# A transposed copy of the lower 16x16 inverse, made once on ScalarE, in the 32x32 inverses of a gated DeltaNet mixer

## The chip, the cores and the metric

The kernel runs on one core of a Trainium2 chip. The metric is the device time of one execution in microseconds (us). The core has five engines, each with its own queue, worked off strictly in order: PE (TensorE, the matmuls), DVE (VectorE), ACT (ScalarE), POOL (GpSimd) and SP, which here only issues DMAs. An instruction whose inputs are not there yet holds up everything behind it on its engine.

## The reference

One encoder layer for two sequences, of 2048 and 512 tokens. The input projection is cut into four mixers (spatial gating, gated DeltaNet, attention, pooling), each is gated, and an output projection follows. The change sits in the DeltaNet mixer. For every chunk of 64 tokens, head and direction, that mixer needs the inverse of a unit lower triangular matrix:

```python
lower = jnp.where(strict, jnp.einsum("bnhid,bnhjd->bnhij", k_beta, k) * decay, 0.0)
t_mat = lax.linalg.triangular_solve(lower + eye, jnp.broadcast_to(eye, lower.shape),
                                    left_side=True, lower=True, unit_diagonal=True)
u = t_mat @ v_beta
w = t_mat @ (k_beta * jnp.exp(g)[..., None])
...
def step(state, xs):
    w_c, u_c, q_c, k_c, a_c, gl_c = xs
    v_new = u_c - w_c @ state
    out = q_c @ state + a_c @ v_new
    state = state * jnp.exp(gl_c)[..., None, None] + jnp.einsum("bhcd,bhce->bhde", k_c, v_new)
    return state, out
```

## The kernel before

The 2560 tokens are worked in five blocks of 512, each of four tiles of 128. `phase1` projects and convolves. Then three things share the engines: the DeltaNet (`deltanet`), the rest of the projections (`phase2`, two passes, matmuls named `accq`, `accz` and `accu`), and, once the pools of the DeltaNet's front are free, attention with the output projection (`phase3`). The program is written unit by unit, and a scheduler with a timeline of its own then sets one order for each engine, by priorities (the DeltaNet's is high) and by when it thinks things are ready. So a change in one place can move rows far behind it, on every engine.

The DeltaNet of a block runs like this, with a tile of 128x128 couplings for each head and direction:

- `pre` (lines 1070 to 1133), once per tile: PE makes the decay exponents `gp` (L1095, L1099) and the key products `kk` (L1110), ACT takes the exponential into `dt` (L1102), DVE makes the couplings `nl` (L1114) and the scaled `dt` (L1116). The 32x32 diagonal blocks go out to DRAM as `dg`. POOL finishes the part `at` (L1131).
- `lanes` (lines 1135 to 1165), once per block: the 128 diagonal blocks of 32x32 are loaded back so that each partition holds one of them, flattened to 1024 values, in the tile `lnl` (`nf`, seen as `nl[p, a, b]`). The inverse grows in the tile `lx` (`xf`, seen as `xt`), which POOL first sets to the identity (L1146, L1147). All products are the helper `dot`: one DVE multiplication into `ltmp` (L1153) and one DVE reduction along the last axis (L1154). First the two 16x16 inverses on the diagonal grow in 15 steps. Then the block `z` that couples them is made: 4 dots that multiply rows of couplings (from `lnl`) with rows of the upper inverse, and 4 dots that multiply the result with the lower inverse, both operands from `lx`. These last four have 1024, 768, 512 and 256 products. A DMA writes the result to DRAM as `xl` (L1165).
- `levels` (from line 1168), twice per block: loads `xl` (L1179), turns it (L1183, L1191), and merges 32x32 blocks to 64 and 128 with small matmuls.
- `step` (in `recurrence`): the state recurrence. Forward and backward direction are two independent chains per sequence. On DVE a step shows as L1289 to L1291, L1296, L1302, L1307, L1314 and L1284.

The upper right quarter of `nl`, `nl[:, 0:16, 16:32]`, is loaded with the rest but no dot reads it: couplings there are zeros.

Two norms feed the same queues: `norm_sums` (L613, L616), whose reciprocal root is POOL's (`rsqrt_pool`, L66 to L71, split at L92), and `norm_turn` (L626).

Of the kernel before, what the change touches and what calls it, by code (L numbers as in the profile page):

```python
# [10 lines left out]
AF = mybir.ActivationFunctionType  # L11
# [33 lines left out]
class Trunk:  # L45
# [1022 lines left out]
    def front(self, dp, dq):  # L1068

        nc = self.nc  # L1070
        V, A, G, PE = nc.vector, nc.scalar, nc.gpsimd, nc.tensor
# [63 lines left out]
        def lanes(tds):  # L1135
            L = len(tds) * 16
            b = tds[0][0] // 4
            done.append(b)
            nf = dp.tile([128, 1056], F32, tag="lnl", name="lnl", bufs=1)
            xf = dp.tile([128, 1056], F32, tag="lx", name="lx", bufs=1)  # L1140
            sq = lambda t: t[:, 0:1024].rearrange("p (a b) -> p a b", b=32)
            halves = lambda t: t.rearrange("p (h x) -> p h x", x=528)[:, :, 0:512].rearrange(
                "p h (a b) -> p h a b", b=32)[:, :, :, 0:16]
            nl, xt, nh, xh = sq(nf), sq(xf), halves(nf), halves(xf)
            nc.sync.dma_start(nf[:, 0:1024], self.DG[b])
            G.memset(xf, 0.0)  # L1146
            G.memset(xf[:, 0:1024:33], 1.0)  # L1147

            def dot(out, x, y, shape):
                tmp = dp.tile([128, 1024], F32, tag="ltmp", name="ltmp", bufs=1)  # L1150
                n = shape[1] * shape[2] * shape[3]
                t = tmp[:, 0:n].rearrange("p (a b c) -> p a b c", a=shape[1], b=shape[2])
                V.tensor_tensor(t, x.to_broadcast(shape), y.to_broadcast(shape), op=ALU.mult)  # L1153
                V.tensor_reduce(out, t, axis=AX.X, op=ALU.add)  # L1154


            for i in range(1, 16):
                dot(xh[:, :, 0:i, i], xh[:, :, 0:i, 0:i], nh[:, :, i:i + 1, 0:i], [128, 2, i, i])
            z = xt[:, 0:16, 16:32]
            for k in range(0, 16, 4):  # L1160
                dot(z[:, k:k + 4, :], nl[:, 16:32, k:16].unsqueeze(1), xt[:, k:k + 4, k:16].unsqueeze(2), [128, 4, 16, 16 - k])
            for k in range(12, -4, -4):
                w = xt[:, 16:20 + k, 16 + k:20 + k].rearrange("p b a -> p a b")
                dot(z[:, :, k:k + 4], w.unsqueeze(1), z[:, :, 0:k + 4].unsqueeze(2), [128, 16, 4, k + 4])
            nc.sync.dma_start(self.XL[b], xf[:, 0:1024])  # L1165

        def levels(t):
# [70 lines left out]
            for d, Pr, Sr in ends:  # L1238
# [5 lines left out]
                for j in range(2):  # L1244
                    nc.sync.dma_start(self.TT[t + j][d], t16[:, :, j * 4:j * 4 + 4].rearrange("p i u f -> p i (u f)"))

        return pre, lanes, levels


# [236 lines left out]
```

## Time and profile before

| | us |
|---|---|
| three timed runs | 1581.16, 1572.33, 1577.47 (median 1577.47) |
| the profiled execution, its own time | 1574.01 |
| its span, first to last instruction | 1572.2 |
| 0 to 340: `phase1` | PE 317.20 busy of 340 |
| 340 to 840: the five `lanes`, with `phase2` beside them | PE 427.10, DVE 405.70 busy of 500 |
| 840 to 1093: end of the recurrence, begin of attention | PE 227.36, DVE 210.82 busy of 253 |
| 1093 to 1500: attention and output projection | PE 386.56, DVE 311.21 busy of 407 |

How to read it: a busy time close to a stretch's length says that the engine sets the pace there, or that it is nearly full. Where no engine is full, the pace is set by waits of one queue for another; such a row shows its idle time and what ended it in brackets, `[2.36 <-DVE dt L1116]`.

### The profile page before, as it was taken

The numbers are of one execution on the slowest core, as the hardware profiler recorded it, in microseconds if no ns is written. First come the engines' busy times: TensorE is split into PE (matmuls) and PEld (weight loads), VectorE is DVE, ScalarE is ACT, GpSimd is POOL, SyncE is SP. The second block draws the span as 40 slices with busy tenths as digits, with TensorE's granted clock in tenths as the row PEclk, the third lists the DMA queues.
The fourth block names the chain that finished last, engine by engine and source line by source line (L and its number), as shares of the span: only waits on it lengthen the run. The fifth ranks groups of instructions, "written<-read, shape, count | busy, mean of one in ns | idle before, by whom it ended". The sixth has DMA issues, their size and how long they took to land. (4 is left out here: it accounts for less than half of the span.)

```text
span 1572.2 us, 34743 instructions
## 1 busy us (share of the span) xinstructions
PE 1425.8 (91%) x13420; PEld 783.5 (50%) x13420; DVE 1173.3 (75%) x2265; ACT 797.0 (51%) x1655; POOL 546.7 (35%) x646
## 2 busy tenths in 40 slices
PE   6999999988989887987889879998799999999898
PEld 3456555543444443544445435555355555555443
DVE  6338579967969887996957769998877887877611
ACT  5244444545454844554546215565567675576400
POOL 3220220044748643455453435555121221121100
PEclk9999999998899989989999999999799999999999
DMA  9845643556566877657689885644411501414332
GB/s 254 283 168 168 190 151 114 150 194 193 160 186 201 258 234 218 199 171 215 186 259 311 278 255 177 202 139 148 161 48 39 173 34 65 160 33 135 114 128 107
DMA packets 250830, 269.65 MB, mean 172 GB/s; under 512 B 95784, under 2 KB 176680, under 8 KB 250024
## 3 DMA queue, kind: packets, MB, share of 16 engines
q1 hardware_dynamic: 250264, 267.36, 54.1%
q8 instruction: 105, 1.72, 0.4%
q14 instruction: 61, 0.50, 0.1%
q0 software_dynamic: 400, 0.07, 0.1%
HBM read 175.66 MB, written 91.77 MB: 170 GB/s over the span
## 5 line engine op out<-in xcount | busy, mean ns | idle before, releaser
L127 PEld LDWEIGHTS <-w 128*128 128x128 f16 x2280 | 223.5, 101 | 307.5 <-issue 81.8
L127 PE MATMUL accz<-xs,w 128*128 128x512 f16 x960 | 243.7, 402 | 16.8 <-DMA xs<-xs 6.7
L958 PE MATMUL op<-wo,mx 128*128 128x512 f16 x960 | 225.3, 379 | 1.0 <-DVE y L962 1.0
L886 DVE TENSOR_REDUCE mm<-mp 128x1 f32<-128x512 f32 x272 | 179.5, 683 | 52.4 <-PE mp L884 52.1
L916 POOL TENSOR_TENSOR p<-e,p 128x512 f16<-128x512 f32 x68 | 86.7, 1274 | 318.6 <-ACT p L915 283.7
L912 ACT ACTIVATE e<-sp 128x512 f32<-128x512 f32 x272 | 153.4, 596 | 79.3 <-PE sp L910 72.9
L916 DVE TENSOR_TENSOR p<-e,p 128x512 f16<-128x512 f32 x204 | 165.8, 828 | 19.3 <-ACT p L915 19.1
L127 PE MATMUL acc<-xs,w 128*128 128x512 f16 x720 | 162.8, 383 | 3.8 <-POOL xs L291 1.5
L915 ACT ACTIVATE p<-e 128x512 f16<-128x512 f32 x272 | 161.2, 632 | 3.4 <-PE O L921 2.0
L921 PEld LDWEIGHTS <-p 128*128 128x128 f16 x3264 | 128.1, 97 | 55.8 <-DVE p L916 11.2
L921 PE MATMUL O<-vt,p 128*128 128x65 f16 (+1 forms) x3264 | 142.6, 193 | 7.5 <-DVE p L916 5.3
L958 PEld LDWEIGHTS <-mx 128*128 128x128 f16 x960 | 91.3, 98 | 104.4 <-issue 1.8
L884 PE MATMUL mp<-ka,qa 128*128 128x512 f16 x272 | 98.7, 395 | 17.3 <-DVE mm L886 10.6
L909 PE MATMUL sp<-qa,ka 128*128 128x512 f16 x272 | 103.9, 384 | 2.6 <-ACT e L912 1.2
L306 DVE SCALAR_TENSOR_TENSOR cv<-raw,convw,cv 128x512 f32<-128x512 f32 x120 | 88.0, 754 | 21.2 <-POOL raw L382 20.6
L910 PE MATMUL sp<-qb,kb 65*128 65x512 f16 x272 | 100.5, 387 | 1.2 <-ACT qb L894 1.0
L127 PE MATMUL accq<-xs,w 128*128 128x512 f16 x360 | 89.5, 391 | 9.9 <-DMA xs<-xs 7.0
L400 PE MATMUL acct<-wtm,xs 128*128 128x400 f16 x480 | 83.8, 332 | 1.9 <-ACT ba L408 0.9
L1268 POOL TENSOR_TENSOR kd<-kv,kds 128x512 f16<-128x512 f32 x40 | 46.9, 1179 | 108.0 <-PE up L1305 56.0
L291 POOL TENSOR_TENSOR xs<-xt,xs 128x512 f16<-128x512 f32 x36 | 49.1, 1386 | 73.5 <-ACT xs L288 73.2
L962 DVE SCALAR_TENSOR_TENSOR y<-op,xr 128x512 f32<-128x512 f32 x40 | 27.5, 687 | 59.2 <-PE op L958 59.1
L127 PE MATMUL accu<-xs,w 128*128 128x512 f16 x240 | 60.9, 403 | 7.2 <-DVE s L616 7.0
(316 smaller groups left out, 2506.8 us busy)
## 6 DMA issues: line engine op xcount, KB each, us to landing
xs<-xs SPq DMA_DIRECT2D x120, 256.0 KB
kx<-kx SPq DMA_DIRECT2D x80, 256.0 KB
at<-at SPq DMA_DIRECT2D x80, 256.0 KB
tt<-tt SPq DMA_DIRECT2D x80, 256.0 KB
xt<-in_xT SPq DMA_DIRECT2D x40, 256.0 KB
xs<-xs SPq DMA_DIRECT2D x5, 2048.0 KB
kv<-kv SPq DMA_DIRECT2D x40, 256.0 KB
mix<-mixs SPq DMA_DIRECT2D x40, 256.0 KB
```

Source lines behind the costliest of these rows:

```text
L127: mm = self.nc.tensor.matmul(ps, w[:, a, k, :], xk, start=k + i == 0, stop=k == 7 and i == 2)
L306: V.scalar_tensor_tensor(cv, raw[:, ct, i:i + 512], self.convw[:, ct, i:i + 1], cv, op0=ALU.mult, op1=ALU.add)
L400: PE.matmul(acc[:, 0:400], xs[:, a, k, tt * 128:(tt + 1) * 128], w[:, c, k, :], start=n == 0, stop=n == 23)
L884: PE.matmul(mp, qa[:, qt * 128:qt * 128 + 128], KA[h // 2][:, sc * 512:sc * 512 + 512], start=True, stop=True)
L886: V.tensor_reduce(mm[:, qt, sc:sc + 1], mp, axis=AX.X, op=ALU.max)
L909: PE.matmul(sp, KA[kv][:, c], qa, start=True, stop=False)
L910: PE.matmul(sp, KB[kv][:, c], qb, start=False, stop=True)
L912: A.activation(e, sp, AF.Exp)
L915: A.activation(p[:, 0], e, AF.Copy)
L916: (G if st % E8 == 1 else V).tensor_tensor(p[:, 1], e, p[:, 0], op=ALU.subtract)
L921: mm = PE.matmul(O[:, qt, 0:z - a], p[:, w, q], v[:, a:z], start=st == 0 and qt == 0 and i == 0, stop=st == nst - 1 and i == 2, skip_group ...
L958: PE.matmul(op, mix[k][:, a, tt * 128:tt * 128 + 128], wo[k][:, c, n * 512:n * 512 + 512], start=i + j == 0, stop=i == 7 and j == 2)
```

## The change

After the four dots that make the first half of `z`, one ACT instruction copies the lower 16x16 inverse, transposed, into the unused quarter of `nl`. The four dots behind it then read the copy `w2` along its rows instead of reading `xt` down its columns. It happens once per block, five times in all.

```diff
             for k in range(0, 16, 4):
                 dot(z[:, k:k + 4, :], nl[:, 16:32, k:16].unsqueeze(1), xt[:, k:k + 4, k:16].unsqueeze(2), [128, 4, 16, 16 - k])
+
+            w2 = nl[:, 0:16, 16:32]
+            A.activation(w2, xt[:, 16:32, 16:32].rearrange("p b a -> p a b"), AF.Copy)
             for k in range(12, -4, -4):
-                w = xt[:, 16:20 + k, 16 + k:20 + k].rearrange("p b a -> p a b")
+                w = w2[:, k:k + 4, 0:4 + k]
                 dot(z[:, :, k:k + 4], w.unsqueeze(1), z[:, :, 0:k + 4].unsqueeze(2), [128, 16, 4, k + 4])
             nc.sync.dma_start(self.XL[b], xf[:, 0:1024])
```

Behind the new lines the line numbers of the changed kernel are higher by three (L1102 stays, L1186 becomes L1189).

ACT in the first of the five blocks, before. The rows belong to `pre` of the following block, and `zz` is a gate of `phase2`:

```order
L1130 ACTIVATE at_4906<-dt 128x512
L606 ACTIVATE zz<-accz 128x512
L1102 ACTIVATE dt<-gp,lcj 128x128 x8
L1130 ACTIVATE at_4962<-dt 128x512
L1126 ACTIVATE dg<-nl 32x128 x4
```

The same place after:

```order
L1130 ACTIVATE at_4907<-dt 128x512
L606 ACTIVATE zz<-accz 128x512
L1102 ACTIVATE dt<-gp,lcj 128x128 x8
L1164 ACTIVATE lnl<-lx 128x16x16
L1130 ACTIVATE at_4963<-dt 128x512
L1126 ACTIVATE dg<-nl 32x128 x4
```

The copy stands between the exponentials and a row that waits for DVE; nothing else moved. In the first three blocks DVE's rows keep their places too; only the names of what four rows read change.

From the fourth block on, rows move on all engines. DVE at the beginning of the fifth `lanes` (rows of `lx` and `ltmp`), with the norms and rotations of `phase2` and steps of the recurrence beside it, before:

```order
L1302 TENSOR_TENSOR v_7486<-up,v_7486 128x256
L1153 TENSOR_TENSOR ltmp<-lx,lnl 128x2
L1154 TENSOR_REDUCE lx<-ltmp 128x2
L616 TENSOR_SCALAR s<-ssp 128x16
L697 TENSOR_TENSOR rt<-q,cs 128x512
L1153 TENSOR_TENSOR ltmp<-lx,lnl 128x8
L66 TENSOR_SCALAR r<-s 128x16
L1307 SCALAR_TENSOR_TENSOR S<-up,S 128x256
L699 TENSOR_TENSOR q<-q,cs 128x512
L700 TENSOR_TENSOR q<-q,rt 128x512
L1154 TENSOR_REDUCE lx<-ltmp 128x2x2
```

and after:

```order
L1153 TENSOR_TENSOR ltmp<-lx,lnl 128x2
L1154 TENSOR_REDUCE lx<-ltmp 128x2
L1305 TENSOR_TENSOR v_7489<-up,v_7489 128x256
L1153 TENSOR_TENSOR ltmp<-lx,lnl 128x8
L1154 TENSOR_REDUCE lx<-ltmp 128x2x2
L1153 TENSOR_TENSOR ltmp<-lx,lnl 128x18
L1154 TENSOR_REDUCE lx<-ltmp 128x2x3
L1153 TENSOR_TENSOR ltmp<-lx,lnl 128x32
L1154 TENSOR_REDUCE lx<-ltmp 128x2x4
L1186 STREAM_TRANSPOSE tnd<-d_8203 128x256
```

The dots of the fifth block have moved ahead of the norm's `s` and the rotations.

DVE some hundred rows later, behind the last `lanes`, with the recurrence's two directions side by side (`S`, `o`, `s` of each), gates (`gz`) and the weights of the output projection (`wo`), before:

```order
L1302 TENSOR_TENSOR v_8560<-up,v_8560 128x256
L1307 SCALAR_TENSOR_TENSOR S<-up,S 128x256 x2
L607 SCALAR_TENSOR_TENSOR gz<-gz,accz 128x512 x2
L1314 SCALAR_TENSOR_TENSOR o<-up,o 128x256
L860 SCALAR_TENSOR_TENSOR wo_12964<-wst,wo_12964 128x1024
L768 SCALAR_TENSOR_TENSOR gz<-ld,psc,gz 128x512
L1314 SCALAR_TENSOR_TENSOR o<-up,o 128x256
```

and after:

```order
L1305 TENSOR_TENSOR v_8564<-up,v_8564 128x256
L860 SCALAR_TENSOR_TENSOR wo_12969<-wst,wo_12969 128x1024
L860 SCALAR_TENSOR_TENSOR wo_12974<-wst,wo_12974 128x1024
L607 SCALAR_TENSOR_TENSOR gz<-gz,accz 128x512
L1310 SCALAR_TENSOR_TENSOR S<-up,S 128x256
L1292 TENSOR_TENSOR o<-up,neg_275 128x256
L1293 TENSOR_TENSOR kv_8610<-o,kv_8610 128x256
L768 SCALAR_TENSOR_TENSOR gz<-ld,psc,gz 128x512
L1294 TENSOR_TENSOR o<-up,eg_273 128x256
```

Before, the two directions update `S` in one go and both gates stand behind them; after, the directions alternate, and a gate stands ahead of the update. On PE the last matmul of the recurrence stands 469 rows earlier than before (row 13568 instead of 14037), with 602 instead of 768 of the attention's `O` matmuls ahead of it, while the first attention matmul stands 294 rows later (row 9902 instead of 9608).

## Prediction

> **What bounds the kernel now.** I read the page's busy times first, then the table by stretches, cut at the five `lanes` (first dot to the write of `xl`), then what PE waits for inside them.
>
> ```profile
> PE 1425.8 (91%) x13420; PEld 783.5 (50%) x13420; DVE 1173.3 (75%) x2265; ACT 797.0 (51%) x1655; POOL 546.7 (35%) x646
> ```
>
> Over the whole span PE is the fullest engine, so a shorter DVE instruction can bring something only where PE waits, directly or through others, for DVE. The stretches (length, then busy time of PE, its weight loads, DVE, ACT, POOL, then granted clock and DMA):
>
> ```profile
> 378.00:431.00 53.00, 47.82 (x242) 22.63 (x241) 50.13 (x98) 27.20 (x70) 32.77 (x44) 0.93 0.49 147
> 452.00:514.00 62.00, 52.37 (x621) 27.84 (x622) 59.73 (x106) 34.15 (x79) 44.81 (x57) 0.92 0.51 162
> 555.00:621.00 66.00, 52.16 (x478) 27.52 (x477) 59.39 (x117) 32.27 (x79) 30.12 (x37) 0.91 0.68 214
> 628.00:699.00 71.00, 64.06 (x839) 36.95 (x838) 66.02 (x140) 38.42 (x93) 35.31 (x55) 0.90 0.57 171
> 734.00:788.00 54.00, 47.02 (x571) 25.97 (x571) 52.26 (x93) 23.60 (x44) 26.51 (x37) 0.94 0.54 164
> 340.00:840.00 500.00, 427.10 (x4545) 226.51 (x4545) 405.70 (x799) 274.20 (x643) 264.69 (x373) 0.91 0.68 208
> 840.00:1093.00 253.00, 227.36 (x2828) 132.88 (x2827) 210.82 (x367) 123.65 (x246) 129.67 (x130) 0.97 0.67 214
> 1093.00:1500.00 407.00, 386.56 (x3957) 217.22 (x3956) 311.21 (x557) 247.07 (x462) 79.70 (x61) 0.97 0.29 97
> ```
>
> In the five `lanes` together DVE is busy 50.13 + 59.73 + 59.39 + 66.02 + 52.26 = 287.5 of 306 us, 94%; PE only 263.4, 86%. There DVE sets the pace. In 340 to 840 as a whole it is busy 81% and PE 85%: between the `lanes` other waits decide. From 1093 on PE is at 95% and takes over: what PE gains before that, it keeps to the end.
>
> That PE waits for DVE there is seen in its own rows; each of these stands behind one or more of the dots that the change shortens:
>
> ```profile
> 426.98 0.38 PE L1095 MATMUL gp<-negf,id 128*128 128x512 f16 x1 [2.36 <-DVE dt L1116]
> 512.85 0.39 PE L1095 MATMUL gp<-negf,id 128*128 128x512 f16 x1 [1.52 <-DVE dt L1116]
> 617.15 0.38 PE L1095 MATMUL gp<-negf,id 128*128 128x512 f16 x1 [0.91 <-DVE dt L1116]
> 692.85 0.39 PE L626 MATMUL turned<-id,r 128*12 128x128 f16 x4 [2.42 <-POOL r L92]
> 784.31 1.89 PE L127 MATMUL accu<-xs,w 128*128 128x512 f16 x8 [1.98 <-DVE s L616]
> ```
>
> **The dots.** The change keeps the number of DVE instructions and of products. What changes is how the last four multiplications of a block read one operand: now down a column, 32 numbers (128 bytes) apart, later along a row. The trace has both kinds in the same sizes, 20 of each: the first four dots of `z` read a row of `lnl` against a row of `lx`, with inner lengths of 16, 12, 8 and 4, as the last four will after the change. First the column readers (`lx` alone), then the row readers (`lnl,lx`):
>
> ```profile
> L1153 DVE TENSOR_TENSOR ltmp<-lx 128x1024 f32<-128x1024 f32 (+3 forms) x20 | 29.9, 1496 | 0.2
> L1153 DVE TENSOR_TENSOR ltmp<-lnl,lx 128x1024 f32<-128x1024 f32 (+3 forms) x20 | 19.0, 949 | 0.2
> 498.11 1.95 DVE L1153 TENSOR_TENSOR ltmp<-lx 128x1024 f32<-128x1024 f32 x1
> 612.51 1.46 DVE L1153 TENSOR_TENSOR ltmp<-lx 128x768 f32<-128x768 f32 x1
> 617.01 1.03 DVE L1153 TENSOR_TENSOR ltmp<-lx 128x512 f32<-128x512 f32 x1
> 697.37 0.59 DVE L1153 TENSOR_TENSOR ltmp<-lx 128x256 f32<-128x256 f32 x1
> 585.19 1.23 DVE L1153 TENSOR_TENSOR ltmp<-lnl,lx 128x1024 f32<-128x1024 f32 x1
> 588.76 0.95 DVE L1153 TENSOR_TENSOR ltmp<-lnl,lx 128x768 f32<-128x768 f32 x1
> 403.39 0.68 DVE L1153 TENSOR_TENSOR ltmp<-lnl,lx 128x512 f32<-128x512 f32 x1
> 601.23 0.41 DVE L1153 TENSOR_TENSOR ltmp<-lnl,lx 128x256 f32<-128x256 f32 x1
> ```
>
> By the two groups the saving is 29.9 - 19.0 = 10.9 us. But some of these rows were held up, and a held-up row need not get shorter:
>
> ```profile
> 423.43 1.25 POOL L644 TENSOR_TENSOR sh<-sg 64x512 f32<-64x512 f32 x1 [2.08 <-ACT dg L1126]
> 423.71 1.36 DVE L1153 TENSOR_TENSOR ltmp<-lx 128x256 f32<-128x256 f32 x1
> ```
>
> The dot of 256 products took 1.36 us here instead of 0.59, and about one microsecond of it lies under a POOL row. So the floor comes from the undisturbed rows: (1.95 - 1.23) + (1.46 - 0.95) + (1.03 - 0.68) + (0.59 - 0.41) = 1.76 us a block, 8.8 us in five. DVE saves 8.8 to 10.9 us; I take 9, near the floor. The Trainium skill, page "SBUF — State Buffer", section "Who interferes with whom", says that a DVE instruction with two SBUF inputs and a GpSimd instruction that reads SBUF exclude each other until the first is done. By that rule the hold-ups stay and the saving is the floor; by a rule of plain slowing it would be the 10.9. The two rows just shown agree with the first.
>
> **The copy.** ACT gets five instructions more, 128x256 in fp32, reading 128 bytes apart. No such row exists. The nearest is one of the same 256 elements along rows, 0.41 us; below that I see no reason, and if a column costs ACT what it costs DVE for the dot of 256 (0.59 to 0.41), it is 0.6 us. I take 0.5, together 2.5 us, all of it on an engine that is half idle. What counts is whether the dots wait for it. The copy can start when the last of the 15 steps has been reduced, and the first column reader comes later:
>
> ```profile
> L1195 ACT ACTIVATE tn<-d 32x256 f32<-32x256 f32 x20 | 8.2, 412 | 1.7 <-DMA d<-xl 1.4
> 396.33 0.62 DVE L1154 TENSOR_REDUCE lx<-ltmp 128x30 f32<-128x450 f32 x1
> 408.75 2.19 DVE L1153 TENSOR_TENSOR ltmp<-lx 128x1024 f32<-128x1024 f32 x1
> 405.15 0.63 ACT L1130 ACTIVATE at<-dt 128x512 f16<-128x512 f32 x1 [9.69 <-DVE dt L1116]
> 669.21 1.06 ACT L1242 ACTIVATE tt<-tt 128x1024 f16<-128x1024 f32 x1 [1.48 <-DMA tt<-tt]
> ```
>
> In the first block 408.75 - 396.95 = 11.8 us lie between, and ACT's order puts the copy into the 9.69 us that it idles ahead of `at`. The wait that the change adds is over long before DVE comes to it, and behind the copy on ACT stands a row that waits for DVE anyway: cost nothing. In the fourth block ACT has no such hole: behind the copy stand `z` of `levels` and eight exponentials, and the delay of 0.4 to 0.6 us ends at the idle 1.48 us before 669.21. Five times without any cover the copy would cost its 2.5 us and no more. I take 0.
>
> `lnl` is now needed until the last dot, not only until the fourth of `z`, and the next block's load may not overwrite it earlier. The tightest case is the fourth block's load:
>
> ```profile
> 618.80 1.32 DVE L1153 TENSOR_TENSOR ltmp<-lx 128x256 f32<-128x256 f32 x1
> 623.44 0.38 SPq L1145 DMA_DIRECT2D lnl<-dg  x1
> ```
>
> The last reader ends at 620.12, the load goes out 3.3 us later: cost nothing.
>
> **How much of 9 us reaches PE.** Per block I take the smaller of PE's idle time in the rows above and of what the dots ahead of it save: 1.76 (of 2.36); 1.52 (three dots ahead, 1.58); 0.91; 0.72 (only the first dot is ahead of the norm whose root POOL makes); 1.58 (of 1.98). Sum 6.5 us. Behind some of these waits another one is nearly as late, since POOL and ACT rows end there too; I take 5. It can't fall below 0 by itself, and 10.9 is the ceiling.
>
> **The order.** The rows for the third `lanes` and before are the old ones, so those terms are clean. From the fourth on the scheduler has placed rows anew: the recurrence finishes earlier on PE, attention begins later there, and on DVE the two directions no longer go in pairs. From 1093 on the rows are nearly the old ones, PE's total work is the same, so only idle time can change. Between 840 and 1093 that is 253 - 227.36 = 25.6 us, and between 340 and 840 it is 72.9 us. I take 0 for the move, with bounds from the rivals below.
>
> Sum: 1574.0 (the profiled execution's own time, 1572.2 span and 1.8 around it) - 5 = 1569.0. The median of the runs shown is 3.5 us higher than this execution; for a median I forecast 1569.0 + 3.5, rounded **1572**. About 0.5%, 7.9 us, is what a measurement of this kernel can tell from no change, and 5 us is less than that.
>
> **Rivals.** *Everything passes and the new order helps.* For it: DVE is 94% busy in the `lanes`, so all 9 to 10.9 us could shorten them, and the earlier dots release `xl`, `levels` and the steps too. And the old order has a knot that the new one unties:
>
> ```profile
> 820.46 0.84 DVE L1307 SCALAR_TENSOR_TENSOR S<-up,S 128x256 f32<-128x256 f32 x2 [2.70 <-PE up L1305]
> 826.36 1.28 DVE L607 SCALAR_TENSOR_TENSOR gz<-gz,accz 128x512 f32<-128x512 f32 x2 [5.05 <-ACT gz L606]
> 827.10 5.78 PE L127 MATMUL accz<-xs,w 128*128 128x512 f16 x19 [3.76 <-DVE gz L607]
> 849.82 0.75 DVE L1307 SCALAR_TENSOR_TENSOR S<-up,S 128x256 f32<-128x256 f32 x2
> ```
>
> There DVE waits 2.70 us for both directions' matmuls, then 5.05 for a gate, and PE loses 3.76. Against it: DVE's gaps between the `lanes` (94.3 - 18.5 = 76 us in 340 to 840) are other waits, which can take up a gain. With all 10.9 and up to 8 from untied knots: 1577.5 - 9 to 1577.5 - 19, so 1558 to 1568.
>
> *The new order costs more than the dots save.* Mechanism: recurrence steps stand closer on PE, while the chain of one step (matmuls, DVE, ACT, matmuls, DVE) needs its time. Above, two updates lie 29.4 us apart (820.46 to 849.82). The new order takes 166 of the attention's `O` matmuls, 42 projection and 25 score matmuls from ahead of the recurrence's last one. Their price by the page:
>
> ```profile
> L921 PE MATMUL O<-vt,p 128*128 128x65 f16 (+1 forms) x3264 | 142.6, 193 | 7.5 <-DVE p L916 5.3
> L127 PE MATMUL accz<-xs,w 128*128 128x512 f16 x960 | 243.7, 402 | 16.8 <-DMA xs<-xs 6.7
> L909 PE MATMUL sp<-qa,ka 128*128 128x512 f16 x272 | 103.9, 384 | 2.6 <-ACT e L912 1.2
> ```
>
> 166 x 142.6/3264 + 42 x 243.7/960 + 25 x 103.9/272 = 7.3 + 10.7 + 9.6 = 27.6 us of PE, over some 13 pairs of steps 2 us a pair. If the chain can't be that much quicker, PE, in order, waits in front of steps that aren't ready, with attention queued behind. From about 0.4 us a pair on it eats the 5 us; at 1 to 2 us a pair, 13 to 26 us less 5, the time is 1585 to 1598. For it: 2.70 us of waiting for such matmuls above. Against it: the old chain has slack, as the knot shows.
>
> *The dots don't get shorter.* If the price came from reading both operands in one tile, or from the shape of the product, and not from the column, row readers would cost 1496 ns on average too: no change, 1577, and up to 2.5 more for the copies. Against it: the first dots of `z` have the same inner lengths, but they also mix two tiles, as the new ones will. So either cause goes. "VectorE: DVE Perf Modes", section "Mode 1× (REGULAR) — the baseline", in the Trainium skill gives this rival its rule: fp32 with odd strides runs at one result per cycle, no slower. The trace disagrees, 1.95 against 1.23 us; the skill's SBUF page, section "Door 1: The DMA port swizzle", has fp32 reads pay from four elements' stride on, which fits.
>
> **Chances.** The forecast, half of the saving through and a neutral order, 45%: 1568 to 1577. All passes and the order helps, 29%: 1558 to 1568. The order costs, 21%: 1580 to 1598. No shorter dots, 5%: 1577 to 1580. The range leaves out about one in ten at either side: 1557 to 1590. Faster than 1569.6: the second case and a small part of the first, 33%. Slower than 1585.4: most of the third, 16%. Within: 51%.
>
> **What would show it.** Right: the four dots at 1.23, 0.95, 0.68 and 0.41 us (mean near 0.95, held-up ones above), no idle DVE row ahead of them that names ACT, copies of 0.4 to 0.6 us, the PE waits in the first three `lanes` smaller by 1 to 2 us each. Wrong: `lanes` as long as before with new waits for POOL in them, or PE idle time between 700 and 1093 that grows or falls by more than 10 us: then the order decides, not the dots.

## The result, and the profile after

The changed kernel took 1560.5 us (median of 7 runs, 1557.5 to 1565.2), the kernel before 1572.4 us (7 runs, 1568.7 to 1581.2). The ratio is **0.9913**, 95% interval 0.9893 to 0.9933: faster by 0.9%, 12 us by the medians and 14 by the ratio. The profiled execution of after took 1564.48 us, 9.5 us less than that of before. One profiled execution differs from the next of the same kernel by some microseconds, so sizes below are those of the timed ratios, and traces are used for the places. Two executions that were slow from end to end, one of 1786 us with the order alone and one of 2807 us of before, are left out of the ratios of the experiments.

Page of after, span and busy times:

```profile
span 1562.7 us, 34751 instructions
PE 1418.7 (91%) x13420; PEld 782.8 (50%) x13420; DVE 1173.4 (75%) x2265; ACT 800.5 (51%) x1660; POOL 537.2 (34%) x646
```

DVE is as busy as before (1173.4 against 1173.3 us) although the dots became shorter: other rows of DVE take longer in the new order. PE's busy time fell by 7.1 us for the same 13420 matmuls, so some of them ran faster; its idle time fell by only 2.4 us, from 146.4 to 144.0. The totals don't say where, nor which of the two is the cause. The stretches give the places (same columns as before):

```profile
340.00:840.00 500.00, 426.02 (x4547) 225.46 (x4546) 407.73 (x811) 277.84 (x649) 257.48 (x378) 0.91 0.69 211
840.00:1093.00 253.00, 221.84 (x2748) 129.90 (x2747) 214.07 (x373) 118.70 (x237) 132.12 (x130) 0.99 0.69 220
1093.00:1500.00 407.00, 396.15 (x4102) 224.91 (x4101) 314.10 (x552) 252.62 (x472) 78.28 (x60) 1.00 0.29 97
```

Between 340 and 840 us almost nothing moved. Between 840 and 1093 us PE is idle 5.5 us longer than before. Between 1093 and 1500 us, where the prediction saw the old rows and a nearly full PE, PE now works 396.2 of 407 us instead of 386.6, and does 145 matmuls more. The page's slices had the place all along. First before, then after (40 slices of 39 us; PE's busy tenths, then the granted clock's):

```profile
PE   6999999988989887987889879998799999999898
PEclk9999999998899989989999999999799999999999
```

```profile
PE   6999999988988887998988888889999999999998
PEclk9999999998998889899999999999999999999999
```

In the slice that begins at 1100 us before has a 7 in both rows; after has a 9 in both. And PE's last projection matmuls, first in before and then in after:

```profile
1127.96 0.81 PE L127 MATMUL accu<-xs,w 128*128 128x512 f16 x3
1118.72 0.81 PE L127 MATMUL accu<-xs,w 128*128 128x512 f16 x3
```

They come 9.2 us earlier, of 9.5 us for the whole execution. So the gain is made by then, and what follows takes as long as before.

The dots of `z` in after (groups by line: busy time, mean ns, idle time ahead), and the copy in the rows of one tile (shortest, median and longest ns, first and last start):

```profile
L1153 DVE TENSOR_TENSOR ltmp<-lnl,lx 128x1024 f32<-128x1024 f32 (+3 forms) x40 | 39.9, 997 | 0.5
```

```profile
L1164 ACT ACTIVATE lnl<-lx x5: 636/652/672, 402.3 to 756.4; 128x256 f32<-128x256 f32 x5
```

All 40 dots of `z` now read rows: 39.9 us instead of 29.9 + 19.0 = 48.9. The copies take 0.65 us each, and no row waits for one.

### The profile page after: what moved, and what is told of

It reads as the page before. It is cut to its first block, busy times and chain, and to the rows that moved or that the text cites. A ratio compares the mean times of both kernels' runs of the same rounds, so it can differ in the third digit from the quotient of the medians.

```text
span 1562.7 us, 34751 instructions
## 1 busy us (share of the span) xinstructions
PE 1418.7 (91%) x13420; PEld 782.8 (50%) x13420; DVE 1173.4 (75%) x2265; ACT 800.5 (51%) x1660; POOL 537.2 (34%) x646
## 5 line engine op out<-in xcount | busy, mean ns | idle before, releaser
L127 PE MATMUL accz<-xs,w 128*128 128x512 f16 x960 | 239.4, 399 | 15.0 <-DMA xs<-xs 5.0
```

What stands on the lines that cost most here:

```text
L127: mm = self.nc.tensor.matmul(ps, w[:, a, k, :], xk, start=k + i == 0, stop=k == 7 and i == 2)
```

## Experiments

All times are compared with runs of before on the same chip, made between them; microseconds more or less are worked out from the ratio.

### The dots and the order apart

The change does two things: other reads, and another order of all rows from the fourth block on. The scheduler doesn't look at how an operand is read, so the two can be had one by one.

The reads alone. The dots take rows of `nl`'s lower right quarter, which needs no copy. These are other numbers than the inverse needs, so this kernel's result is not the layer's; the counts and shapes are those of before, and so is the order on every engine:

```diff
-                w = xt[:, 16:20 + k, 16 + k:20 + k].rearrange("p b a -> p a b")
+                w = nl[:, 16 + k:20 + k, 16:20 + k]
```

> The order of before on every engine, without the copy: the last four dots of a block read a row of couplings in lnl instead of a column of lx (the result of the coupling block is another one, since a wrong operand is multiplied; counts and shapes are those of before). The row readers should cost what the first four dots cost, a mean near 0.95 us instead of 1.50, 9 to 11 us less DVE time. Theory A (the dots bring the gain): nearly all of it comes here, ratio to before 0.991 to 0.994, 9 to 14 us. Theory B (the new order brings it): 0.997 to 1.000, at most 5 us. Theory C (both, about half each): 0.994 to 0.997.

Measured: 1568.9 us against 1572.7, ratio 0.9976 [0.9960, 0.9992], 3.8 us less. DVE spends 40.9 us on the dots, 8.0 less.

The order alone: the change, but the copy is made and not read; the dots read `xt` down its columns as before.

```diff
-                w = w2[:, k:k + 4, 0:4 + k]
+                w = xt[:, 16:20 + k, 16 + k:20 + k].rearrange("p b a -> p a b")
```

> The order of after on every engine with the five copies made, but the dots read down the column of lx as before, so nothing gets shorter on DVE. Theory A (dots): 0.999 to 1.003. Theory B (order): 0.991 to 0.994. Theory C: 0.994 to 0.998. If both E1 and this one fall short of the gain, the two act only together.

Measured: 1563.5 us, 0.9938 [0.9915, 0.9962], 9.8 us less.

The other sign: in before, the first four dots of `z` read columns too (again other couplings than the right ones).

```diff
-                dot(z[:, k:k + 4, :], nl[:, 16:32, k:16].unsqueeze(1),
+                dot(z[:, k:k + 4, :], nl[:, 16 + k:32, 0:16].rearrange("p b a -> p a b").unsqueeze(1),
                     xt[:, k:k + 4, k:16].unsqueeze(2), [128, 4, 16, 16 - k])
```

> The order of before, and the first four dots of a block read columns too, of lnl (other couplings than the right ones are multiplied; counts and shapes unchanged). Their mean should rise from 0.95 to about 1.50 us, 9 to 11 us more DVE time in the five blocks. If the blocks pass on DVE time one to one (theory A), the kernel is 9 to 12 us slower, ratio 1.006 to 1.008; if other waits take it up (theory B), 1.000 to 1.003.

Measured: 1582.4 us, 1.0065 [1.0042, 1.0089], 10.2 us more, for 29.9 + 27.6 - 48.9 = 8.6 us more in DVE's dots.

The whole change once more, beside these:

> The changed kernel once more, on the same chip and beside the same runs of before as the three others: 0.991, between 0.989 and 0.993, by every theory. By theory A it stands at E1's ratio, by theory B at E2's, by theory C at the product of both.

Measured: 1559.8 us, 0.9917 [0.9891, 0.9942]. The parts multiply to the whole: 0.9976 x 0.9938 = 0.9914. **So the order brings some 10 of 13 to 14 us, the dots some 4.**

### Which piece of the new order

Built with the copy in the fourth block alone, the program has the order of the changed kernel on PE, DVE, POOL and SP; built with the copy in any one other block, it has that of before. So one ACT row in the fourth block set off the whole move. From here on an order is written out by hand: the instructions are those of before, without a copy and with column reads, and each gets an edge of order alone, without a wait, to the one that is to stand ahead of it on its engine:

```diff
         Trunk(tc, NP, NS, ins, outs).run()
+        fixed_order(tc, nc, _mybir)
...
+        for x in a[k + 1:k + 1 + n]:
+            at += x
+            if last is not None:
+                tc.add_manual_dep(by[f"I-{at}"], last, info(), reason="issue_after")
+            last = f"I-{at}"
```

(`a` holds the instruction numbers of one engine after the other, `info()` makes an edge without a wait.) Any head of one schedule can be followed by what is left, in the order of the other. Four such mixtures, cut at the fifth load of `lnl` (about 725 us) and at the first score matmul (about 910 us):

> The instructions of before, none added and none changed, with the order on every engine set by hand: as in the changed kernel up to the fifth load of lnl (from about 690 to 725 us; 35 SP rows, 58 DVE rows and 350 matmuls stand elsewhere than before), and what is left then in the order of before. Theory F (the gain of the new order comes in this first piece, where the fifth load goes out 15.6 us behind the fourth xl write instead of 24.5): about 9 us below before, ratio 0.994, and the gap 15 to 17 us. Theory M (it comes between that load and the first score matmul, the fifth lanes and the recurrence without attention): ratio 1.000. Theory L (it comes behind the first score matmul, where recurrence and attention share PE): 1.000 too, and the gap is short all the same.

> The counterpart: the instructions of before, in the order of before up to the fifth load of lnl, and from there in the order of the changed kernel (771 DVE rows stand elsewhere than before). F: 0 to 1 us below before, ratio 0.9995, the gap 24 us as before. M or L: 8 to 10 us below, 0.994. If the pieces add up, this and the run beside it together give 10 us.

> The same instructions, in the order of the changed kernel up to the first score matmul (about 910 us), and what is left in the order of before. F: 9 us below before, 0.994, as the run that changes only the piece ahead of the load. M: 9 us below as well, while that run shows nothing. L: nothing, 1.000, and the stretch of half clock near 1100 us that before shows is still there.

> The same instructions, in the order of before up to the first score matmul, and from there in that of the changed kernel. F and M: 1.000. L: 8 to 10 us below before, 0.994, with a mean granted clock of 0.966 instead of 0.961 and no half clock near 1100 us.

Measured: new until the load 0.9999 [0.9982, 1.0015]; new from the load 0.9938 [0.9919, 0.9957]; new until attention 1.0006 [0.9991, 1.0022]; new from attention 0.9955 [0.9929, 0.9982]. Theories F and M fall, L stands: **the gain lies behind 910 us**. The first run of the four tests less than it said: the load itself fell behind the cut, and it goes out 24.6 us after the `xl` write, as in before. The run with the new order until attention settles F (its DMA issues):

```profile
708.47 1.05 SPq L1165 DMA_DIRECT2D xl<-lx  x1
723.65 0.45 SPq L1145 DMA_DIRECT2D lnl<-dg  x1
```

Its load goes out 15.2 us behind `xl`, as early as in after (15.6), and it gains nothing. Neither does the order in which the recurrence's two directions go before attention begins.

### What the old order costs there

In the trace of before (all engines, in order of time), behind the last step of the recurrence:

```profile
1100.80 0.69 DVE L1333 TENSOR_REDUCE om<-osq 128x8 f32<-128x512 f32 x1 [2.50 <-ACT osq L1332]
1101.40 0.68 DVE L886 TENSOR_REDUCE mm<-mp 128x1 f32<-128x512 f32 x1
...
1102.14 0.58 PE L884 MATMUL mp<-ka,qa 128*128 128x512 f16 x1 [3.27 <-DVE mm L886]
...
1109.04 0.59 PE L884 MATMUL mp<-ka,qa 128*128 128x512 f16 x1 [0.78 <-DVE mm L886]
...
1109.67 0.69 DVE L886 TENSOR_REDUCE mm<-mp 128x1 f32<-128x512 f32 x1
...
1110.41 0.59 PE L884 MATMUL mp<-ka,qa 128*128 128x512 f16 x1 [0.78 <-DVE mm L886]
...
1111.03 0.69 DVE L886 TENSOR_REDUCE mm<-mp 128x1 f32<-128x512 f32 x1 [0.68 <-PE mp L884]
...
1114.11 0.58 PE L892 MATMUL mr<-id,m 128*1 128x128 f16 x4
```

Attention takes a maximum of each piece of scores first: PE makes the scores (`mp`), DVE reduces them (`mm`), and the next `mp` waits for that. From one to the next it takes 1.37 us, of which PE works 0.59. Elsewhere scores, `O` and projection matmuls of the work beside it fill the gap. Here they are used up: the `O` matmuls of all scores made so far stand ahead of the recurrence's end, and 15 of the last 24 projection matmuls (`accu`) too. So PE stands idle between 1097 and 1113 us, nine times and 9.0 us together, and from 1102 to 1122 us the clock is granted at half. The longest wait, 3.27 us, has a cause of its own: on DVE, L1333, from the norm behind the recurrence, waits for ACT and holds up a maximum behind it. ACT in turn waits for a load, the recurrence's output on its way back from DRAM:

```profile
1100.14 0.63 ACT L1332 ACTIVATE osq<-ob 128x512 f32<-128x512 f32 x1 [2.73 <-DMA ob<-od]
```

In after that load goes out at 1074.2 us instead of 1096.7, with other work still beside it.

The same time in after (PE's rows):

```profile
1090.18 0.38 PE L884 MATMUL mp<-ka,qa 128*128 128x512 f16 x1
1090.40 0.38 PE L909 MATMUL sp<-qa,ka 128*128 128x512 f16 x1
1090.62 0.38 PE L910 MATMUL sp<-qb,kb 65*128 65x512 f16 x1
1090.84 0.38 PE L884 MATMUL mp<-ka,qa 128*128 128x512 f16 x1
1091.05 2.75 PE L127 MATMUL accz<-xs,w 128*128 128x512 f16 x12
1093.64 0.38 PE L921 MATMUL O<-vt,p 128*128 128x65 f16 x7
1093.86 0.38 PE L884 MATMUL mp<-ka,qa 128*128 128x512 f16 x1
```

Between two maxima stand scores, `O` and projection matmuls, no wait is left, and matmuls of 512 take 0.38 us instead of 0.59. Behind the recurrence's last matmul 51 projection matmuls are still to come, not 9.

The Trainium skill, page "TensorE: Matmul & The Clock Gate", section "HAM oscillation — how this bites in real kernels", has the clock fall to half when PE is idle for more than about 3.4 us. The 3.27 us wait with 0.58 us matmuls right behind it agrees, nearly. That suggests that the half clock is what costs. Three kernels ask: one that puts work into the gap, and two other orders that the scheduler itself makes when the copy goes to another engine.

```diff
-            A.activation(w2, xt[:, 16:32, 16:32].rearrange("p b a -> p a b"), AF.Copy)
+            G.tensor_copy(w2, xt[:, 16:32, 16:32].rearrange("p b a -> p a b"))
```

(for DVE `V.tensor_copy`; for the first kernel, 15 PE rows of before's order change places.)

> The instructions of before in the order of before on DVE, ACT, POOL and SP. On PE alone 15 accu matmuls move: from ahead of the last step of the recurrence (1092.6 and 1095.2 us) to behind the maxima (L884, mp), where PE now waits for DVE's reduction of each: three to four at a time between 1097 and 1102 us, then two behind each of the last four maxima. Theory K (the stretch from 1097 to 1113 us, where the maxima alternate between PE and DVE, is what the old order costs, and the granted clock of 0.50 from 1100 to 1120 us follows from PE being half idle there): the 15 fill 3 to 6 us of the waits and cost up to 2 us of new waiting where they stood, the half clock becomes shorter; 2 to 8 us below before, ratio 0.995 to 0.999, waits for mm from 8.6 to 3 to 5 us. Rival P (the stretch is not on the path, or the clock falls by itself): ratio 1.000 and half the clock from 1100 to 1120 us as before.

> The whole change, with the copy on POOL instead of ACT. The scheduler makes a third order of it. In that one the last maxima stand as in before: behind the last step of the recurrence come two, four transposes, two, eight transposes, nine maxima and then the rows mr, with no O, score or projection matmul between. K: only the dots' gain is left, ratio 0.997 to 0.999, PE's waits for mm at 7 to 10 us in 900 to 1180 us, half clock near 1100 us. P (orders differ by things that have nothing to do with this stretch): any ratio from 0.988 to 1.003, with no tie to those waits.

> The whole change, with the copy on DVE. A fourth order: around the last step of the recurrence the maxima stand among scores, O and projection matmuls, and 121 projection matmuls are left behind it (9 in before, 51 in the changed kernel). K: the gain of the order is there, 9 to 10 us, the dots bring 3.5 us less what five copies cost DVE (about 3 us): ratio 0.991 to 0.995, waits for mm at 2 to 4 us, no half clock near 1100 us. P: any ratio from 0.988 to 1.003.

Measured: filled 0.9995 [0.9974, 1.0015]; copy on POOL 1.0042 [1.0025, 1.0059]; copy on DVE 0.9978 [0.9963, 0.9993]. The stretch from 1090 to 1130 us in before, in the filled kernel, with the copy on POOL, with the copy on DVE, and in after (columns as before):

```profile
1090.00:1130.00 40.00, 29.57 (x235) 14.54 (x234) 32.16 (x67) 13.68 (x27) 8.82 (x9) 0.74 0.56 180
```

```profile
1090.00:1130.00 40.00, 28.70 (x240) 13.68 (x237) 34.12 (x70) 15.84 (x30) 8.84 (x9) 0.91 0.59 188
```

```profile
1090.00:1130.00 40.00, 34.48 (x311) 17.47 (x312) 33.73 (x70) 15.58 (x31) 8.48 (x7) 0.83 0.50 166
```

```profile
1090.00:1130.00 40.00, 39.83 (x391) 22.71 (x389) 35.00 (x64) 25.45 (x47) 4.97 (x4) 1.00 0.55 185
```

```profile
1090.00:1130.00 40.00, 39.26 (x405) 22.02 (x404) 38.77 (x71) 27.75 (x53) 9.81 (x8) 1.00 0.52 171
```

Filling brought the clock from 0.74 to 0.91 (two other kernels with this tail untouched, rows alone and the last one below, show 0.83) and no time that can be seen; up to 4 us stay possible by the interval. The waits for `mm` fell from 8.6 to 6.4 us, less than K said. The rows say why:

```profile
1098.47 0.63 ACT L1332 ACTIVATE osq<-ob 128x512 f32<-128x512 f32 x1 [4.37 <-DMA ob<-od]
1100.47 0.38 PE L884 MATMUL mp<-ka,qa 128*128 128x512 f16 x1 [3.64 <-DVE mm L886]
1104.64 0.59 PE L884 MATMUL mp<-ka,qa 128*128 128x512 f16 x1 [1.04 <-DVE mm L886]
1106.01 0.59 PE L884 MATMUL mp<-ka,qa 128*128 128x512 f16 x1
```

This execution was 1.5 us ahead already (L1288 at 1090.48 instead of 1092.00). Rid of the 15 matmuls, the recurrence's last step then starts 3.5 us earlier (L1300 at 1093.03 instead of 1096.48). But ACT has its load only 1.7 us earlier, and the longest wait grows from 3.27 to 3.64 us: next to nothing of the 2 us won is left. So work moved from just ahead of the gap into it mostly moves the idle time: PE was busy for 28.7 us of 40, in before for 29.6. The maxima still follow each other 1.37 us apart, still at half clock (0.59 us); the clock comes back only behind them. So this kernel bounds the price of the half clock that it took away, 4 us at most, but doesn't show what the maxima alone would cost at full clock. Theory K was right on the clock and failed on the time.

The two orders of the scheduler came out on the sides that K named, POOL's with the maxima alone, DVE's without, but both about 0.5% slower than it said, and POOL's waits for `mm` are 4.9 us, not 7 to 10. Both lose ahead of the tail. Two rows of 700 to 900 us, with the copy on POOL and on DVE:

```profile
700.00:900.00 200.00, 162.07 (x2035) 89.81 (x2033) 149.71 (x257) 91.69 (x183) 86.76 (x100) 0.91 0.76 237
```

```profile
700.00:900.00 200.00, 162.82 (x2173) 94.05 (x2172) 148.87 (x279) 88.06 (x178) 101.18 (x131) 0.89 0.76 231
```

PE works 162 to 163 us there, against 68.11 + 103.88 = 172.0 in before (its rows of 700 to 780 and 780 to 900) and 172.0 in after: some 9 us of PE's time. With the copy on DVE PE also works 14 us less between 340 and 700 (295.2 against 309.5 us). Both get part of it back between 900 and 1093 (3.5 and 6.7 us more than before). This was seen only in the traces and not tried by itself, so what these two orders lose, and why, stays open.

The last kernel puts the old tail, and only that, behind the new order:

> The instructions of before, in the order of the changed kernel up to the 33rd of the 36 state updates (about 1060 us), and what is left then in the order of before: from the matmuls that stand at 1083 us in before on, PE's order is that of before row by row, with the last steps, the maxima alone between PE and DVE, and all but 9 projection matmuls used up. Theory K' (the gain of the new order is PE's idle time in that last piece, 1097 to 1113 us, and not the half clock in it, since 15 matmuls put there brought the clock back and no time): ratio 0.998 to 1.002, waits for mm at 7 to 10 us in 900 to 1180 us, PE busy for 28 to 32 of the 40 us from 1090 to 1130 us. Theory Q (the gain comes between 910 and 1060 us, where recurrence and attention share PE, and the maxima have no part in it): ratio 0.993 to 0.996 in spite of those waits.

Measured: 1574.8 us against 1573.6, 1.0015 [0.9994, 1.0035]: Q falls, K' stands. With three state updates left, the whole gain of the order is still to be won or lost. Nor is it the clock: the mean granted clock is 0.965 in this kernel and in the filled one, as in after. The fair partner is the kernel with columns and copy unread, which goes on in the new order. PE's busy time in all is 1417.5 us with the old tail and 1415.9 there, its idle time 155.3 and 145.4; 9.7 us of that difference lie between 1093 and 1500 us. The old tail's rows:

```profile
1104.21 0.58 PE L884 MATMUL mp<-ka,qa 128*128 128x512 f16 x1 [2.93 <-DVE mm L886]
...
1111.12 0.58 PE L884 MATMUL mp<-ka,qa 128*128 128x512 f16 x1 [0.78 <-DVE mm L886]
```

The kernels side by side, with PE's busy time from 1093 to 1500 us and its waits for `mm` between 900 and 1180 us:

| order behind 1060 us | kernel | PE busy of 407 | waits for `mm` | ratio |
|---|---|---|---|---|
| old | before | 386.6 | 8.6 | 1 |
| old | new until load | 386.8 | 8.3 | 0.9999 |
| old | new until attention | 383.6 | 10.3 | 1.0006 |
| old | new, old tail | 385.0 | 9.3 | 1.0015 |
| old, gap filled from ahead | filled | 386.1 | 6.4 | 0.9995 |
| old, row readers | rows alone | 386.1 | 7.6 | 0.9976 |
| old, more columns | more columns | 384.7 | 8.2 | 1.0065 |
| new | new from load | 393.3 | 3.2 | 0.9938 |
| new | new from attention | 393.8 | 2.3 | 0.9955 |
| new | columns, copy unread | 394.7 | 3.2 | 0.9938 |
| new, row readers | after | 396.2 | 2.9 | 0.9913 |
| new, row readers | after, again | 394.6 | 2.7 | 0.9917 |
| a third | copy on POOL | 389.0 | 4.9 | 1.0042 |
| a fourth | copy on DVE | 395.4 | 2.7 | 0.9978 |

The last two fences of this kind, with the old tail and with the new order from attention on:

```profile
1093.00:1500.00 407.00, 384.96 (x4010) 217.83 (x4007) 313.60 (x561) 247.20 (x463) 81.46 (x63) 0.98 0.30 98
```

```profile
1093.00:1500.00 407.00, 393.77 (x4098) 223.90 (x4097) 316.46 (x556) 254.28 (x476) 78.73 (x60) 1.00 0.29 96
```

In the three kernels with the new tail and column reads PE is busy 6.7 to 8.1 us longer there than in before; the order's 0.45 to 0.62% are 7 to 10 us. The last two rows don't follow, since they lose elsewhere. That the order behind 1060 us decides is shown by the mixtures: new from attention wins, and the old tail takes all of it away. (The new tail behind an old head up to 1060 us was not run.) That the load, the norm and the lone maxima are the whole of its cost is read from the traces: the only kernel that changed PE's rows there alone left the idle time as it was.

## Why the prediction was right and where it was wrong

The time lies in the range, 1560.5 in 1557 to 1590, and that is in part luck: 5 us less were forecast and 12 to 14 came, and the term that brought most of them had been taken as 0. (The 3.5 us on top, for the median, came from three runs of before; seven have 1572.4, and less 5 us that is 1567.) It is below the 1572 of the likeliest case and in the span of the second one, 1558 to 1568, whose total fits and whose parts do not: the dots brought less than its 10.9 us, and the order brought its 8 us and more at another place.

- *The dots.* Taken: 9 us on DVE. Measured: 8.0 with the reads alone, a little under the floor of 8.8, and 9.0 in after. Near the floor was the right price, and the hold-ups stayed: the 256-product dots average 0.69 us in after, not the 0.41 of an undisturbed one; by their medians the four sizes take 1.22, 0.95, 0.69 and 0.43 us, as said. (The held-up row quoted for it ended 0.39 us behind POOL's row, less than the 0.59 of an undisturbed one. So it was held up, but not shut out for the whole of POOL's row.) "The dots don't get shorter" fell.
- *The copy.* Taken: 0.5 us, cost nothing. Measured: 0.65 us, above the upper estimate of 0.6, and nothing waits for it. A column costs ACT a little more than the DVE ratio said. `lnl`'s longer use shows no cost: in the tightest case the load goes out 4.9 us behind the last dot.
- *The pass-through.* Taken: 5 us. Measured: 3.8 us, interval 1.3 to 6.3. PE's five quoted waits, 9.2 us together before, are these in after:

```profile
431.47 0.38 PE L1095 MATMUL gp<-negf,id 128*128 128x512 f16 x1 [1.53 <-DVE dt L1116]
516.16 0.39 PE L1095 MATMUL gp<-negf,id 128*128 128x512 f16 x1 [0.22 <-DVE dt L1116]
621.59 0.38 PE L1095 MATMUL gp<-negf,id 128*128 128x512 f16 x1 [0.92 <-DVE dt L1116]
697.30 0.39 PE L626 MATMUL turned<-id,r 128*12 128x128 f16 x4 [1.77 <-POOL r L92]
783.45 5.12 PE L127 MATMUL accu<-xs,w 128*128 128x512 f16 x23 [0.91 <-DVE s L616]
```

  Sum 5.4, 3.8 us less, in one execution. Of the first three, which were to shrink by 1 to 2 us each, one did (1.3 us), one shrank by 0.8, and one stayed.
- *The order.* Taken: 0. Measured: 10 us. **This is the step that failed**, and in it the sentence "From 1093 on the rows are nearly the old ones, PE's total work is the same, so only idle time can change. Between 840 and 1093 that is 253 - 227.36 = 25.6 us, and between 340 and 840 it is 72.9 us". The search for idle time stopped at 1093, because PE was busy 95% behind it. But 95% of 407 us leaves 20 us, and half of them stood together at 1097 to 1113. And the rows behind 1093 were not the old ones: 51 projection matmuls instead of 9 were left for them. The prediction had counted that 42 projection matmuls move behind the recurrence, as work that the recurrence is rid of, and did not ask what they would fill.
- *The second case's knot* at 820 us brought nothing: new until attention, which has the new order there, gives 1.0006. *The third case*, a chain that can't keep up with steps standing closer, didn't come: new from attention is faster.
- *The mark set for being wrong*, PE's idle time between 700 and 1093 us changing by over 10 us, did not show: it grew by 4.6 us (345.0 to 340.4 busy of 393), while the order decided. The mark ended where the search had ended.

## What to carry to other kernels

Where a scheduler sets the order, an edit of one row can move thousands; build the order alone and the work alone, and time them apart before crediting the edit. A stretch that is 95% busy on average can still hold a gap that is worth the whole change: read it in slices of 20 to 40 us, and ask of moved work not only what it delays but what gap it now fills. Work put into a gap from just ahead of it moved the idle time and saved nothing that could be measured; before filling a gap, follow its longest wait back to what ends it, here a load.

## Not expected of the hardware

- Some 20 us of half clock in the tail, cut to some 7 in the filled kernel (0.74 and 0.91 on average in 40 us), were worth nothing that could be measured: ratio 0.9995, at most 4 us. Most of the maxima that waited for DVE ran at half clock in both.
- Reading 128 bytes apart, one transposed 16x16 fp32 block per partition (128x256) took 0.65 us on ACT, 0.62 on POOL and 0.38 on DVE (medians of five). One of five was held up on POOL (1.69 us) and one on DVE (2.31), none on ACT.
- More column reads cost about their whole DVE time (10.2 us for 8.6), fewer brought about half (3.8 for 8.0). The intervals (6.6 to 14.0 and 1.3 to 6.3 us) leave open how unequal the two are.
